# The v and attention-value projections as two 1024-column groups with seven block products in five tile pairs

## The chip, the cores and the metric

The kernel runs on one core of one Trainium2 chip. The metric is the device time of one execution, in microseconds (us). Before the change three runs took 1321.61, 1322.16 and 1323.86 us; the median is 1322.16.

The engines are named as the profile names them: PE is TensorE (matrix products), DVE is VectorE, ACT is ScalarE, POOL is GpSimd, and SP is SyncE, whose queue issues the loads of the weights. A letter q behind a name means the engine's issuing queue. An "L" and a number is a line of the kernel.

## The reference

One layer of an encoder over 256 positions with 2048 columns, all in float32:

```
h    = rms_norm(x) ; proj = h @ w_in              # u, v | q, k, va | gates A, B
y_a  = gelu(u) * (w_s @ LN(gelu(v)) + b_s)        # per 128-position chunk, 8 groups
y_b  = neighbourhood_attention(q, k, va)          # 16 heads of 64, 4 x 64 grid, learned bias
m    = sigmoid(gA) * (y_a @ w_branch[:1024]) + sigmoid(gB) * (y_b @ w_branch[1024:])
x    = x + m @ w_out
x    = x + conv_ffn(rms_norm(x))                  # up 2048 -> 11008, conv width 3, SiLU gate, down
out  = rms_norm(x)
```

The columns of `w_in` are u (0 to 1023), v (1024 to 2047), q, k, the attention values va (4096 to 5119), and the two gates of 2048 columns each. The change is about v and va: each is 256 x 2048 times 2048 x 1024.

## The kernel before

**Exact products from three.** A float32 product is made of three float32r matmuls. Each operand is split into a high part (a copy in float32r, by ACT) and a low part (operand minus high part, by DVE), and the product is high x high + low x high + high x low. For activations these parts lie in `h` (x chunks), `m`, `a`; for weights in `whi` and `wlo`. I call the three matmuls a triple.

**Pieces.** The weights of the whole layer are cut into pieces of 512 KB (128 partitions x 1024 values), numbered in the order in which PE uses them. SP loads them into `wraw`, five buffers deep (`LOAD_AHEAD`). `split_to` splits a piece: ACT copies it to `whi`, DVE subtracts for `wlo`, in four buffers each, three pieces ahead of PE (`SPLIT_AHEAD`).

**Order.** Nothing is scheduled by a tool: each engine executes its instructions in the order in which the Python code writes them. `begin(i)` opens piece i. It issues loads up to piece i + 4, writes the split of piece i + 3, and then runs the tasks that stand for i in a table (`at(i, f)`). For i below 5 the tasks come ahead of the splits. Then come the piece's matmuls. A task put at i thus stands behind the split of piece i + 3 and ahead of the split of piece i + 4 on ACT and DVE, and ahead of the matmuls of piece i on PE.

**Start.** x arrives in eight chunks of 256 columns (`load_x`, 256 KB each). `x_chunk(c)` turns one over on PE (four 128x128 transposes, L496), and ACT and DVE split it (L468, L475) into `h`. In the first eight pieces one chunk per piece is turned and used at once. The sums of squares of x (`x_stats`, on ACT) and the norm (`x_norm`) follow at pieces 5 to 9; the norm's factor is applied when a group is finished.

**Groups.** A `natural` group makes 512 output columns: eight pieces, each of two k tiles (k counts the 16 tiles of 128 input columns), for two halves of the positions, 12 matmuls a piece. A `stationary` group makes transposed outputs. A `wide` group makes 1024 columns in 16 pieces, each one k tile by two column halves: 2 x 2 triples a piece. In chosen pairs of k tiles (`quads`) the four sums of two products are made with seven triples instead of eight (a Winograd-type scheme): sums of activations (`act_sums`, L290 to L295, split at L301 and L302) and of weights (`weight_sums`, L308 to L311, split at L318 and L319) take the place of one triple. The weight sums stand at three pieces ahead of their use, their split two ahead. Four further banks P hold block products that are added to several outputs when the last pair is done (L807 to L811 for a gate), and the other four banks C are added when the group ends (L822). PSUM has eight banks in all.

**Before the change** v is two natural groups (pieces 0 to 15), then come u (16 to 31), and va, q and k, and half of the gates in alternating natural and stationary groups, among which the attention's small steps are hung as tasks. v's LayerNorm (`ln_stats`) hangs on pieces 17 and later, beside u. The gates' other halves, w_out and the down-projection are wide groups already.

Of the kernel before, what the change touches and what calls it, by code (L numbers as in the profile page):

```python
# [15 lines left out]
T = 256  # L16
# [26 lines left out]
GATE_QUADS = (1, 3, 5)  # L43
# [4 lines left out]
Y_GAP = 192  # L48
# [4 lines left out]
def trunk_kernel(ctx, tc, x, norm_mix, w_in, ln_g, ln_b, w_s, b_s, rpb, w_branch, w_out,  # L53
# [48 lines left out]
    def load_to(n):  # L102
        while n_loaded[0] < min(n, len(pieces)):
# [58 lines left out]
    midway = {}  # L162

# [66 lines left out]
    def run_group(g, by_block=0):  # L230
# [4 lines left out]
        for i in range(n0, n1 - by_block):  # L235
# [7 lines left out]
            for b in range(nblk):  # L243
                if b == 1 and i in midway:
                    midway.pop(i)()
                products(g, ps, i, b, h, l)
# [13 lines left out]
    def wide(src, row0, order, c0, acts, quads, room, done, sums=None):  # L260
        n0 = plan_wide(src, row0, order, c0)
        boxes = {}
        for q in quads:
            i = n0 + 2 * q
            whole[i] = whole[i + 1] = None
# [8 lines left out]
            at(i - 2, lambda b=b: weight_sums_split(b, room))  # L274
# [49 lines left out]
    def run_wide(g, tail=0):  # L324
# [12 lines left out]
        for i in range(n0, n1 - tail):  # L337
# [162 lines left out]
    yT = [ypool.tile([128, 2, T], F32R, name=f"y{k}") for k in range(KD)]  # L500
    ypool.tile([128, Y_GAP // 4], F32, name="gap")

# [6 lines left out]
    def ev_vg(j):  # L509
        def done(ps, i):  # L510
            if j == 0:
                at(i + 2, lambda: gelu_v(ps, i))
            else:
                gelu_v(ps, i)

        def gelu_v(ps, i):
            G = gm_pool["p"]
            if j == 0:
                gm_pool["v"] = [G.tile([128, GMW], F32, name=f"vg{t}") for t in range(NT)]
                gm_pool["sum"] = const.tile([128, NT, 2], F32, name="vsum")  # L520
            for t in range(NT):
                nc.scalar.activation(gm_pool["v"][t][:, j * 512:(j + 1) * 512], ps[t], AF.Gelu_apprx_tanh,
                                     scale=st1["r"][:, t:t + 1], accum_out=gm_pool["sum"][:, t, j:j + 1])
            if j == 1:
                at(i + 1, ln_stats)
        return done

    def ln_stats():
        i = cur[0]
        mu = const.tile([128, NT], F32, name="mu")  # L530
# [5 lines left out]
        nc.vector.tensor_add(mu, su[:, :, 0], su[:, :, 1])  # L536
        nc.vector.tensor_scalar(nm, mu, -1.0 / GMW, None, op0=OP.mult)
# [70 lines left out]
    def ev_va(j):  # L608
        def done(ps, i):
            A = at_pool["p"]  # L610
            va = A.tile([128, NT, 512], F32, name="va", bufs=1)
            for t in range(NT):
                nc.scalar.activation(va[:, t, :], ps[t], AF.Copy, scale=st1["r"][:, t:t + 1])

            def windows(r):
                for b in range(NBLK):
                    c0 = (r % 2) * 64 + WIN0[b]
                    nc.gpsimd.dma_start(at_pool["v"][r * WIN:(r + 1) * WIN, b, j * 512:(j + 1) * 512],
                                        va[c0:c0 + WIN, r // 2, :])

            for r in range(ROWS):
                at(i + 1 + r // 2, lambda r=r: windows(r))
        return done
# [177 lines left out]
    def ev_gate_sums(br):  # L801
        def done(P, i):
            def go():
                gate_tile(br)
                p1, p5, p6, p7 = P
                g11, g12, g21, g22 = (mg["t", br][:, t, c * 512:(c + 1) * 512] for t in range(2) for c in range(2))
                nc.scalar.activation(g11, p1, AF.Copy)  # L807
# [353 lines left out]
    for g in g_vg:  # L1161
        run_group(g)
# [108 lines left out]
```

## Time and profile before

| | us |
|---|---|
| median of three runs | 1322.16 |
| the profiled execution | 1321.89 |
| its span, first to last instruction | 1319.9 |
| PE busy in the span | 1307.3 (99%) |
| DVE busy | 1030.5 (78%) |
| ACT busy | 755.0 (57%) |
| POOL busy | 101.6 (8%) |

How to read the lines that follow. A row of the order in time has start, length, engine, line, operation, written tile <- read tiles, form, how many were merged (x4), and in brackets how long the engine sat idle before and what ended that. A row of waits has the waiting instruction, what it waited for, us in total, times, and the longest. A row of a stretch has its length and, for PE, weight loads, DVE, ACT and POOL, the busy time and number of instructions, then the granted clock of PE, the share of DMA, and GB/s. A row of a group has busy time and the mean in ns of one.

### The profile page before, as it was taken

The numbers are of one execution on the slowest core, as the hardware profiler recorded it, in microseconds if no ns is written. First come the engines' busy times: TensorE is split into PE (matmuls) and PEld (weight loads), VectorE is DVE, ScalarE is ACT, GpSimd is POOL, SyncE is SP. The second block draws the span as 40 slices with busy tenths as digits, with TensorE's granted clock in tenths as the row PEclk, the third lists the DMA queues.
The fourth block names the chain that finished last, engine by engine and source line by source line (L and its number), as shares of the span: only waits on it lengthen the run. The fifth ranks groups of instructions, "written<-read, shape, count | busy, mean of one in ns | idle before, by whom it ended". The sixth has DMA issues, their size and how long they took to land.

```text
span 1319.9 us, 19273 instructions
## 1 busy us (share of the span) xinstructions
PE 1307.3 (99%) x6791; PEld 1115.5 (85%) x6791; DVE 1030.5 (78%) x1561; ACT 755.0 (57%) x1127; POOL 101.6 (8%) x192
## 2 busy tenths in 40 slices
PE   9999999999999999999999999999999999999997
PEld 7888888888887888888888888888888888888885
DVE  6477667767598966996787878787878779999997
ACT  6565566667554644556655556565555556555653
POOL 0241155530000000000000000000000000000000
PEclk9999999999999999999999999999999999999999
DMA  9766775755666666665656665656566657656663
GB/s 317 231 189 183 216 224 165 218 173 155 199 176 208 200 197 221 219 214 162 191 179 195 184 194 181 202 176 204 180 195 187 192 154 229 220 192 206 212 197 122
DMA packets 174800, 259.37 MB, mean 197 GB/s; under 512 B 12920, under 2 KB 124400, under 8 KB 174704
## 3 DMA queue, kind: packets, MB, share of 16 engines
q1 hardware_dynamic: 170416, 250.31, 60.9%
q0 software_dynamic: 3968, 7.30, 2.2%
q8 instruction: 53, 0.87, 0.3%
q10 hardware_dynamic: 320, 0.53, 0.1%
q14 instruction: 43, 0.35, 0.1%
HBM read 253.90 MB, written 2.10 MB: 194 GB/s over the span
## 4 chain that ended last, share of the span: by engine, by line
PE 98%; DVE 1%; DMA 0%; ACT 0%; issue 0%; SPq 0%; ACTq 0%; DVEq 0%
PE bank L196 31%; PE bank L200 16%; PE bank L285 10%; PE bank L283 10%; PE bank L284 10%; PE bank L224 7%; PE bank L226 7%; PE bank L225 7%; PE bank L722 1%; DMA wraw<-in_w_in_dram 0%; PE bank L772 0%; PE bank L598 0%; PE bank L762 0%; PE bank L933 0%; PE bank L496 0%
## 5 line engine op out<-in xcount | busy, mean ns | idle before, releaser
L144 DVE TENSOR_TENSOR wlo<-wraw,whi 128x1024 fp32r<-128x1024 f32 (+1 forms) x471 | 553.6, 1186 | 225.6 <-ACT whi L143 120.9
L143 ACT ACTIVATE whi<-wraw 128x1024 fp32r<-128x1024 f32 (+1 forms) x471 | 475.3, 1022 | 225.9 <-PE bank L225 72.1
L196 PE MATMUL bank<-h,whi 128*128 128x512 f32 x1760 | 425.2, 392 | 0.0
L196 PEld LDWEIGHTS bank<-h,whi 128*128 128x128 f32 x1760 | 322.5, 189 | 61.6
L200 PEld LDWEIGHTS bank<-h,wlo 128*128 128x128 f32 x1760 | 225.9, 191 | 8.8
L200 PE MATMUL bank<-h,wlo 128*128 128x256 f32 x1760 | 228.6, 283 | 0.0
L958 ACT ACTIVATE tc<-ta,ck 128x256 f32<-128x256 f32 x86 | 47.1, 594 | 117.1 <-DVE ta L956 117.1
L224 PE MATMUL bank<-whi,h 128*128 128x512 f32 x256 | 102.4, 400 | 0.6 <-ACT whi L143 0.6
L285 PE MATMUL bank<-wlo,a 128*128 128x512 f32 x260 | 101.6, 391 | 0.2 <-DVE wlo L144 0.2
L283 PE MATMUL bank<-whi,a 128*128 128x512 f32 x260 | 101.3, 390 | 0.0
L284 PE MATMUL bank<-whi,a 128*128 128x512 f32 x260 | 101.3, 390 | 0.0
L225 PE MATMUL bank<-whi,h 128*128 128x512 f32 x256 | 100.1, 391 | 0.3 <-DVE h L475 0.3
L226 PE MATMUL bank<-wlo,h 128*128 128x512 f32 x256 | 100.2, 391 | 0.0
L285 PEld LDWEIGHTS bank<-wlo,a 128*128 128x128 f32 x260 | 48.8, 188 | 11.3 <-DVE wlo L144 1.3
L284 PEld LDWEIGHTS bank<-whi,a 128*128 128x128 f32 x260 | 48.9, 188 | 10.1
L283 PEld LDWEIGHTS bank<-whi,a 128*128 128x128 f32 x260 | 48.8, 188 | 10.1
L224 PEld LDWEIGHTS bank<-whi,h 128*128 128x128 f32 x256 | 48.3, 189 | 10.4 <-ACT whi L143 1.1
L226 PEld LDWEIGHTS bank<-wlo,h 128*128 128x128 f32 x256 | 48.1, 188 | 10.6 <-DVE wlo L144 0.4
L225 PEld LDWEIGHTS bank<-whi,h 128*128 128x128 f32 x256 | 48.2, 188 | 10.1 <-DVE h L475 0.8
L1234 POOL DMA_DIRECT2D gfin<-in_norm_final_dram x4 | 2.2, 548 | 696.8 <-DVE tc L969 577.3
L961 DVE SCALAR_TENSOR_TENSOR tc<-ta,ck,tc 128x255 f32<-128x255 f32 x86 | 41.4, 481 | 14.4 <-ACT tc L958 14.4
L948 ACT ACTIVATE tb<-bank 128x256 f32<-128x256 f32 x86 | 28.3, 385 | 42.5 <-PE bank L196 42.2
(254 smaller groups left out, 1702.4 us busy)
## 6 DMA issues: line engine op xcount, KB each, us to landing
wraw<-in_w_up_dram SPq DMA_DIRECT2D x336, 256.0 KB, 3.4
wraw<-in_w_in_dram SPq DMA_DIRECT2D x111, 512.0 KB, 4.3
wraw<-in_w_down_dram SPq DMA_DIRECT2D x86, 512.0 KB, 4.7
wraw<-in_w_in_dram SPq DMA_DIRECT2D x66, 256.0 KB, 3.5
wraw<-in_w_branch_dram SPq DMA_DIRECT2D x32, 512.0 KB, 3.9
wraw<-in_w_out_dram SPq DMA_DIRECT2D x32, 512.0 KB, 4.4
xs<-in_x_dram SPq DMA_DIRECT2D x8, 256.0 KB, 7.4
vw<-va POOLq DMA_DIRECT2D x32, 64.0 KB, 5.3
```

The source lines that it names most:

```text
L143: nc.scalar.activation(h[:, k, :m], w[:, k, :m], AF.Copy)
L144: nc.vector.tensor_sub(l[:, k, :m], w[:, k, :m], h[:, k, :m].bitcast(F32))
L196: nc.tensor.matmul(p, h[:, k - k0, b * 128:(b + 1) * 128], acts(k), start=k == 0, stop=k == nk - 1)
L200: nc.tensor.matmul(p[:, :T], l[:, k - k0, b * 128:(b + 1) * 128], acts(k)[:, 0, :], start=False, stop=False)
L224: nc.tensor.matmul(p, xh, h[:, kk, :m], start=st, stop=False)
L225: nc.tensor.matmul(p, xl, h[:, kk, :m], start=False, stop=False)
L226: nc.tensor.matmul(p, xh, l[:, kk, :m], start=False, stop=sp)
L283: nc.tensor.matmul(p, xh, h, start=st, stop=False)
L284: nc.tensor.matmul(p, xl, h, start=False, stop=False)
L285: nc.tensor.matmul(p, xh, l, start=False, stop=sp)
L958: nc.scalar.activation(v, u, AF.Identity, scale=ck[:, 1, ch:ch + 1], bias=ck[:, 3, ch:ch + 1])
L961: nc.vector.scalar_tensor_tensor(v[:, 1:], u[:, :T - 1], ck[:, 0, ch:ch + 1], v[:, 1:], op0=OP.mult, op1=OP.add)
```

## The change

v and va become wide groups of 16 pieces each and run first, one behind the other: v in pieces 0 to 15, va in 16 to 31, u in 32 to 47. v has its seven-product pairs at pieces 10 to 13 (`V_QUADS` 5 and 6), va at 18, 19, 22, 23, 26 and 27 (`VA_QUADS` 1, 3 and 5). The k tiles are taken in another order (`V_ORDER`, `VA_ORDER`), and the x chunks are turned at pieces 0 to 9 in the order of `X_TURN`, 0, 3, 1, 4, 2, 5, 6, 7. The first piece is one k tile, loaded as two column halves, and its first six matmuls use the first half alone. The sums of x chunks 1, 2 and 6 that the pairs need are made at pieces 3, 5 and 20 (`X_SUMS`).

The results of v and va are no longer taken from PSUM by ACT alone: `post_sums` and `add_sums` (DVE) combine the banks in SBUF, and ACT applies Gelu or the norm's factor there. v's LayerNorm falls on pieces 17 to 24. The turning of w_s and of the constants of later stages moves from pieces 14 to 19 to pieces 29 to 31, and the row factor `rb` from 12 to 29. The attention's fill now consists of gate groups; va's windows are copied by POOL in 16 transfers over all columns instead of 32 over half of them. The second gate group gets other pairs and k orders, and one more branch group stands ahead of the attention's end. The number of pieces stays the same.

```diff
-GATE_QUADS = (1, 3, 5)
+V_QUADS, V_ORDER = (5, 6), (0, 1, 6, 7, 8, 9, 10, 11, 12, 13, 2, 3, 4, 5, 14, 15)
+VA_QUADS, VA_ORDER = (1, 3, 5), (0, 1, 2, 3, 6, 7, 4, 5, 8, 9, 12, 13, 10, 11, 14, 15)
+X_TURN = ((0, 0), (3, 1), (1, 2), (4, 3), (2, 4), (5, 5), (6, 7), (7, 9))
+X_SUMS = ((1, 3, 3), (2, 5, 5), (6, 20, 20))
+GATE_PAIRS = (2, 4, 6)
+GATE_QUADS = ((2, 4, 6), (1, 3, 5))
...
             if i == 0:
                 for k in range(kn):
-                    if k:
-                        load_x(256, 256)
-                    nc.sync.dma_start(w[:, k, :cn], src[r0 + k * 128:r0 + (k + 1) * 128, c0:c0 + cn])
+                    nc.sync.dma_start(w[:, k, :cn], src[r0:r0 + 128, c0 + k * step:c0 + k * step + cn])
...
-                for t in range(NT):
-                    for c in range(2):
-                        plain(i, t, c)
+                for t, c in ((0, 0), (0, 1), (1, 0), (1, 1)) if i else ((0, 0), (1, 0), (0, 1), (1, 1)):
+                    plain(i, t, c)
...
+    def post_sums(P, x, spare):
+        p1, p5, p6, p7 = P
+        (x11, x12), (x21, x22) = x
+        nc.scalar.activation(x11, p1, AF.Copy)
+        nc.vector.tensor_add(spare, p6, x11)
+        nc.vector.tensor_add(x12, p5, spare)
+        nc.vector.tensor_add(x21, p7, spare)
+        nc.vector.tensor_add(x22, p5, x21)
+
+    def add_sums(ps, x):
+        for t in range(NT):
+            for c in range(2):
+                nc.vector.tensor_add(x[t][c], ps[t][c], x[t][c])
...
+    def ev_v(ps, i):
+        add_sums(ps, gm_pool["v4"])
...
+        at(i + 1, gelu)
+        at(i + 2, ln_stats)
...
-    g_vg = [natural(w_in2, 0, KD, V0 + j * 512, 512, xt, ev_vg(j)) for j in range(2)]
...
+    g_v = wide(w_in2, 0, V_ORDER, V0, xt, V_QUADS, first_room, (ev_v_sums, ev_v), first_sums,
+               lambda name, dt: s_room["odd"].tile([128, 2, 512], dt, name=name))
+    g_va = wide(w_in2, 0, VA_ORDER, VA0, xt, VA_QUADS, first_room, (ev_va_sums, ev_va), first_sums)
...
-    at(12, lambda: st1.__setitem__("rb", bcast_cols(st1["r"])))
+    at(29, lambda: st1.__setitem__("rb", bcast_cols(st1["r"])))
...
-    at(14, lambda: turn_ws(0))
-    at(15, lambda: turn_ws(1))
+    at(30, lambda: turn_ws(0))
+    at(31, lambda: turn_ws(1))
     preload[13] = [ld for ld, _ in late]
     for n, (_, f) in enumerate(late):
-        at(17 + n // 2, f)
+        at(29 + n // 2, f)
```

How the order moves, on three places. First DVE at the start. `wlo` is the low half of a piece, `h3` to `h5` are x chunks, `y0` and `y6` hold activation sums and their low half. Before, from the split of piece 3:

```order
L144 TENSOR_TENSOR wlo_252<-wraw_153,whi_251 128x1024
L475 SCALAR_TENSOR_TENSOR h4_113<-bank_270,gmix_85,h4_113 128x256 x2
L144 TENSOR_TENSOR wlo_280<-wraw_156,whi_279 128x1024
L475 SCALAR_TENSOR_TENSOR h5_114<-bank_297,gmix_85,h5_114 128x256 x2
L144 TENSOR_TENSOR wlo_307<-wraw_212,whi_306 128x1024
```

Changed, from the split of piece 3 to that of piece 4:

```order
L148 TENSOR_TENSOR wlo_230<-wraw_138,whi_229 128x1024
L291 TENSOR_TENSOR y0_248<-h1_110 128x512
L293 TENSOR_TENSOR y0_248<-y0_248 128x128
L294 TENSOR_TENSOR y0_248<-y0_248 128x128
L295 TENSOR_TENSOR y0_248<-y0_248 128x128
L296 TENSOR_TENSOR y0_248<-y0_248 128x128
L303 TENSOR_TENSOR y6_254<-y0_248,y6_254 128x512
L475 SCALAR_TENSOR_TENSOR h4_113<-bank_257,gmix_85,h4_113 128x256 x2
L148 TENSOR_TENSOR wlo_267<-wraw_141,whi_266 128x1024
```

Six instructions moved in between two splits; a second set stands between the split of piece 8 and chunk 5. The next place is DVE behind the split of piece 17 (`vg` is v, `y0` and `y1` the weight sums, `wsT` the turned w_s). Before:

```order
L144 TENSOR_TENSOR wlo_554<-wraw_533,whi_553 128x1024
L1153 COPY wsT_138<-bank_557 128x512
L144 TENSOR_TENSOR wlo_578<-wraw_551,whi_577 128x1024
L1153 COPY wsT_138<-bank_581 128x512
L144 TENSOR_TENSOR wlo_604<-wraw_575,whi_603 128x1024
```

Changed, from the split of piece 17 over the half split of piece 18 to the first of the last adds:

```order
L148 TENSOR_TENSOR wlo_574<-wraw_553,whi_573 128x1024
L522 TENSOR_TENSOR junk_75<-bank_509,vg0_577 128x512
L523 TENSOR_TENSOR vg0_577<-bank_508,junk_75 128x512
L524 TENSOR_TENSOR vg1_578<-bank_510,junk_75 128x512
L525 TENSOR_TENSOR vg1_578<-bank_508,vg1_578 128x512
L148 TENSOR_TENSOR wlo_599<-wraw_571,whi_598 128x512
L309 TENSOR_TENSOR y0_602<-wraw_571 128x512
L310 TENSOR_TENSOR y1_603<-wraw_596,y0_602 128x512
L311 TENSOR_TENSOR y0_602<-wraw_596,wraw_571 128x512
L312 TENSOR_TENSOR y1_603<-wraw_596,y1_603 128x512
L530 TENSOR_TENSOR vg0_577<-bank_173,vg0_577 128x512
```

The first adds, the weight sums and the last adds (the first of four is shown, then comes the split of piece 19) now stand between these splits. The third place is ACT at v's LayerNorm; `junk` is the target of the squares (L542, now L563), `vg` of the normalisation (L552, now L573). Before, beside u:

```order
L542 ACTIVATE junk_75,vs4_634<-vg0_475,nmu_632 128x512 x2
L143 ACTIVATE whi_666<-wraw_619 128x1024
L542 ACTIVATE junk_75,vs4_634<-vg1_476,nmu_632 128x512 x2
L143 ACTIVATE whi_688<-wraw_664 128x1024
L448 ACT_TABLE_LOAD
```

Changed, beside va; `whi_704` is the half copy of piece 22:

```order
L563 ACTIVATE junk_75,vs4_684<-vg0_577,nmu_682 128x512 x2
L147 ACTIVATE whi_704<-wraw_676 128x512
L563 ACTIVATE junk_75,vs4_684<-vg1_578,nmu_682 128x512 x2
L147 ACTIVATE whi_730<-wraw_702 128x1024
L319 ACTIVATE y2_734<-y0_708 128x1024
L319 ACTIVATE y3_738<-y1_709 128x1024
L302 ACTIVATE y8_748<-y0_742 128x512
```

The squares kept their place between copies, and behind them the copies of the weight sums and the sums of chunk 6 have joined.

More of the change, by code (lines that the diff above doesn't have):

```diff
@@ L255, in run_group, with wide @@
             done(ps, b)
-    def wide(src, row0, order, c0, acts, quads, room, done, sums=None):
+    def wide(src, row0, order, c0, acts, quads, room, done, sums=None, odd=None):
         n0 = plan_wide(src, row0, order, c0)
         boxes = {}
-        for q in quads:
+        for n, q in enumerate(quads):
             i = n0 + 2 * q
+            own = odd if odd and n % 2 else room
             whole[i] = whole[i + 1] = None
@@ L804, in go @@
                 gate_tile(br)
-                p1, p5, p6, p7 = P
-                g11, g12, g21, g22 = (mg["t", br][:, t, c * 512:(c + 1) * 512] for t in range(2) for c in range(2))
-                nc.scalar.activation(g11, p1, AF.Copy)
-                nc.vector.tensor_add(junk, p6, g11)
-                nc.vector.tensor_add(g12, p5, junk)
-                nc.vector.tensor_add(g21, p7, junk)
-                nc.vector.tensor_add(g22, p5, g21)
+                mg["x", br] = [[mg["t", br][:, t, c * 512:(c + 1) * 512] for c in range(2)] for t in range(NT)]
+                post_sums(P, mg["x", br], junk)
             at(i + 1, go)
@@ L1115, in trunk_kernel @@
     at(0, lambda: keep_awake(WAKE[1]))
[L1116 to L1118 removed]
+    for c, i in X_TURN[1:]:
+        at(i, lambda c=c: x_chunk(c))
     xsq = const.tile([128, NT, 4], F32)
```

157 lines of the change are left out of this document (79 added, 78 removed).

## The prediction

> **What bounds the kernel now.** I read the page first (span, busy shares, chain), then what TensorE (PE) waited for, then stretches of the span, and last the order in time of the engines. The page:
>
> ```profile
> span 1319.9 us, 19273 instructions
> ...
> PE 1307.3 (99%) x6791; PEld 1115.5 (85%) x6791; DVE 1030.5 (78%) x1561; ACT 755.0 (57%) x1127; POOL 101.6 (8%) x192
> ...
> PE 98%; DVE 1%; DMA 0%; ACT 0%; issue 0%; SPq 0%; ACTq 0%; DVEq 0%
> ```
>
> TensorE is busy for 99% and carries 98% of the chain that ended last. What it waited for (us in total, times, longest):
>
> ```profile
> PE bank L433 <- POOL ident masks.py:199: 1.4, 1, 1.4
> PE bank L283 <- DVE m L473: 0.9, 1, 0.9
> PE bank L224 <- ACT whi L143: 0.6, 1, 0.6
> PE bank L225 <- DVE h L475: 0.3, 1, 0.3
> ```
>
> The first belongs to the start-up. So a matmul less shortens the run, as long as VectorE (DVE) and ScalarE (ACT) deliver in time. How full DVE is depends on the stage:
>
> ```profile
> 66.00:99.00 33.00, 33.00 (x200) 29.49 (x199) 26.31 (x43) 21.14 (x31) 15.11 (x23) 1.00 0.64 189
> ...
> 429.00:462.00 33.00, 33.00 (x147) 27.35 (x146) 31.31 (x37) 21.03 (x23) 0.00 (x0) 1.00 0.65 200
> ```
>
> The columns after the length are PE, weight loads, DVE, ACT, POOL. In the seven-product gate groups (429 to 462) DVE works 31.3 of 33 us and PE still never waits. That is the closest row to what the change asks for.
>
> **The change, step by step.** *Less on PE.* Five pairs need 7 instead of 8 triples: 5 x 3 = 15 matmuls of 512 columns fewer. Their pace, and the pieces around it:
>
> ```profile
> 8.28 0.51 PE L224 MATMUL bank<-whi,h 128*128 128x512 f32 x1 [0.61 <-ACT whi L143]
> ...
> 14.38 0.60 PE L496 MATMUL bank<-ident,xs 128*128 128x128 f32 x4
> 14.73 0.48 PE L224 MATMUL bank<-whi,h 128*128 128x512 f32 x1
> ...
> 17.60 0.60 PE L496 MATMUL bank<-ident,xs 128*128 128x128 f32 x4
> ...
> 28.32 0.50 PE L225 MATMUL bank<-whi,h 128*128 128x512 f32 x1 [0.29 <-DVE h L475]
> ...
> 28.89 0.39 PE L224 MATMUL bank<-whi,h 128*128 128x512 f32 x1
> ...
> 44.31 0.39 PE L226 MATMUL bank<-wlo,h 128*128 128x512 f32 x1
> ```
>
> From 28.89 to 44.31 lie 68 steps: 0.227 us each, 2.72 for a piece of 12; the four transposes of an x chunk add 0.35 (14.38 to 14.73), and a piece with its chunk takes 3.22 (14.38 to 17.60). Gain: 15 x 0.227 = 3.4. The wait of 0.61 before the second half of piece 0 goes too: six matmuls, not three, now run on the first half, and no x chunk is loaded between the halves. Together **-4.0**. The 0.29 at 28.32 says that an x chunk arrives with no lead at this stage.
>
> *More on DVE and ACT.* Durations, DVE first:
>
> ```profile
> 16.84 1.23 DVE L144 TENSOR_TENSOR wlo<-wraw,whi 128x1024 fp32r<-128x1024 f32 x1
> ...
> 22.30 0.88 DVE L475 SCALAR_TENSOR_TENSOR h<-bank,gmix,h 128x256 fp32r<-128x256 f32 x2 [1.02 <-ACT h L468]
> 23.25 4.63 DVE L144 TENSOR_TENSOR wlo<-wraw,whi 128x1024 fp32r<-128x1024 f32 x4
> ...
> 38.59 0.15 DVE L1128 TENSOR_REDUCE ss<-xsq 128x2 f32<-128x8 f32 x1
> ...
> 40.01 0.16 DVE L453 TENSOR_TENSOR n_r<-n_r,n_s 128x2 f32<-128x2 f32 x1
> ...
> 76.13 1.32 DVE L556 TENSOR_TENSOR vg<-vg,lng 128x1024 f32<-128x1024 f32 x1
> ...
> 78.63 1.32 DVE L144 TENSOR_TENSOR wlo<-wraw,whi 128x1024 fp32r<-128x1024 f32 x1
> ...
> 370.15 0.68 DVE L290 TENSOR_TENSOR t<-h 128x512 f32<-128x512 f32 x1
> ...
> 371.81 1.22 DVE L144 TENSOR_TENSOR wlo<-wraw,whi 128x1024 fp32r<-128x1024 f32 x1
> ...
> 385.84 0.69 DVE L144 TENSOR_TENSOR wlo<-wraw,whi 128x512 fp32r<-128x512 f32 x1
> ...
> 388.98 1.28 DVE L837 TENSOR_TENSOR g<-bank,g 128x512 f32<-128x512 f32 x2
> ...
> 392.51 2.36 DVE L319 TENSOR_TENSOR l<-t,h 128x1024 fp32r<-128x1024 f32 x2
> ...
> 420.30 0.69 DVE L808 TENSOR_TENSOR junk<-bank,g 128x512 f32<-128x512 f32 x1
> ...
> 422.35 0.69 DVE L811 TENSOR_TENSOR g<-bank,g 128x512 f32<-128x512 f32 x1
> ...
> 432.47 2.48 DVE L822 TENSOR_TENSOR g<-bank,g 128x512 f32<-128x512 f32 x4
> ```
>
> ```profile
> 22.15 3.90 ACT L143 ACTIVATE whi<-wraw 128x1024 fp32r<-128x1024 f32 x4
> 25.95 0.83 ACT L468 ACTIVATE h<-bank,gmix 128x256 fp32r<-128x256 f32 x2
> ...
> 63.92 0.73 ACT L542 ACTIVATE junk<-vg,nmu 128x512 f32<-128x512 f32 x1 [3.99 <-DVE nmu L537]
> ...
> 64.77 0.72 ACT L542 ACTIVATE junk<-vg,nmu 128x512 f32<-128x512 f32 x1
> ...
> 72.77 1.25 ACT L552 ACTIVATE vg<-vg,nmr,ln_r 128x1024 f32<-128x1024 f32 x1 [0.76 <-DVE nmr L548]
> ...
> L301 ACT ACTIVATE h<-h 128x512 fp32r<-128x512 f32 x14 | 8.9, 633 | 38.6 <-PE bank L285 18.8 <-DVE h L295 14.4 <-DVE wlo L144 3.2
> ```
>
> Step from one DVE instruction to the next: split of a piece 1.14 ((4.63 - 1.23) / 3), an x chunk 0.80, activation sums 1.66 (370.15 to 371.81) plus 0.60 after ACT's 0.63 copy, a half split with its four weight sums 3.14 (385.84 to 388.98), the split of these sums 2.27, the first adds of a finished group 2.66 (420.30 to 422.35, and 0.61), its last adds 2.40, the norm chain 1.6 (38.59 to 40.17), one affine 2.50. ACT: a copy 0.95 ((3.90 - 1.05) / 3), half a copy 0.54 (0.63 less the same overlap), an x chunk 0.73.
>
> *Piece 4* (first order fence). The activation sums now stand between the splits of pieces 3 and 4, and x chunk 4 waits for them on ACT. Call T the start of the transposes ahead of piece 3. Before, the split of piece 3 ends at T + 0.47 (17.60, and 16.84 + 1.23), and I keep that. The sums end at T + 2.1, ACT's copy of them, chunk 4 and the copy of piece 4 (0.54 + 0.73 + 1.05) at T + 4.4, the low half 1.2 later, T + 5.6. PE wants the high half at T + 3.57 (3.22 + 0.35) and, held up by 0.85 there, the low half at T + 4.95: 0.85 + 0.65 = **+1.5**. Queued behind on both engines are chunk 2 and the splits of pieces 5 to 8.
>
> *Piece 6* is the first that uses x chunk 5, which now stands behind five splits and a second set of sums. From S, the start of piece 4's low half: 1.14 + 0.80 + 4 x 1.14 + 1.74 = 8.25, ACT 0.54 and 0.47: S + 9.3. PE has done pieces 4 and 5 at S + 1.23 + 2.3 + 0.35 + 2.72 = S + 6.6. The delay of 2.7 and another 0.4 for the chunk's low half: **+3.1**.
>
> *Piece 8* needs chunk 6, behind the half split and weight sums of piece 10. ACT comes to that half copy after piece 9's and two squares of x (as long as L542's, 0.85): S + 12.8; with 3.14 and 0.47 the chunk's low half is there at S + 16.5. PE, restarted at S + 10.0, wants it at S + 15.8 (11 matmuls, 0.35, 2.72, one matmul): **+0.7**.
>
> *Pieces 8 to 26* (second and third fence). PE and DVE stand together at chunk 6, without lead. Up to the end of the split of piece 27, which piece 26 needs, DVE has 13 splits 14.8, four half splits with sums 12.6, four splits of sums 9.1, chunks 1.2, norm 1.6, first adds 2.7, last adds 2.4, activation sums with ACT's copy 2.9, LN's small chain 2.0 (norm and two more), two affines 5.0: 54.3. It also waits for ACT: 2.3 where LN's squares (2 x 0.85) and half a copy (0.63) come first, 1.0 where a normalisation does (1.15 + 0.95, less the 1.14 of the split before), and by estimate 0.3 behind x's squares. Sum 57.9. PE has in the same stretch 11 + 12 + 84 (four pairs of 21) + 96 + 5 = 208 matmuls, 47.2, and 0.35 of transposes: 47.6. The lead of three pieces that hides this in the gate groups never builds up here: **+10.3**, most of it before pieces 24 and 26.
>
> *Piece 29* asks for three more of the eight PSUM banks while the group holds all eight; they come free with the third of the first adds. DVE: 2.27 + 4 x 1.14 + 2.05 = 8.9 after that split, PE arrives after 28 matmuls and four transposes, 6.7: **+2.2**.
>
> *Nothing* for attention: its cover is the absence of any PE wait there, and the POOL copies of v are half as many and issued some 30 pieces ahead of their first reader. If late, they would hold the first weighted sum. Gates keep their count of products; with DVE up to 95% full there I bound the moved sums by -0.9 (the wait on L473, if it goes) and +0.9 (if one like it joins), and take 0.
>
> Sum: -4.0 + 1.5 + 3.1 + 0.7 + 10.3 + 2.2 = **+13.8**. The profiled execution took 1321.89 (1319.9 of it in the span), 0.3 below the median 1322.16: 1335.7 on the one, **1336** on the other.
>
> **A rule weighed.** The gate row above shows a DVE at 95% that holds nobody up. The Trainium skill, Perfetto Trace Analysis, "Identifying the Most-Contended Engine", says to take the engine with the highest occupancy and relieve it first. By the whole-run shares that is PE, and the sum would be -4.0; by the same rule read for pieces 8 to 26 it is DVE, 57.9 against 47.6. That page itself warns, under "Optimization Strategy", that the most contended engine changes with the regime; the rows side with that.
>
> **Rivals.** *DVE keeps up* as in the gate groups, and only the gain is left: 1318.2. For it speaks the row at 429 to 462; against it that those groups start with three pieces of lead and carry neither x chunks nor LN. It decides if the shortfalls together fall below 4.0 instead of 17.8. Chance 0.07, of which 0.02 near no change.
> *ACT's waits vanish* because copies slip in while DVE is behind, and piece 29 finds its banks: 1336 - 3.6 - 2.2 = 1330. Chance 0.10.
> *Loads come late*: raw buffers are kept until the sums have read them. Before, a load takes
>
> ```profile
> wraw<-in_w_in_dram SPq DMA_DIRECT2D x111, 512.0 KB, 4.3
> ```
>
> from issue to landing; one of these fully on the path would give 1340. Against: five buffers, and DVE is the later one anyway. Chance 0.08.
> *The clock drops* after the longest wait, some 5 us before piece 26. Before has no such wait, so no row prices it: at half pace the next 28 matmuls would cost 6.4, of which piece 29's 2.2 are swallowed: between 1336 and 1340, I say 1338. Chance 0.11. The Trainium skill, TensorE: Matmul & The Clock Gate, Part 1, gives a window of about 3.4 us of idleness after which the clock halves; by it I estimate 1.7 lost, which piece 29 would swallow. The granted clock is 1.00 in the rows above, and no run here shows such a drop.
>
> **How the numbers follow.** My case has 0.64, at 1336 (5% on the 57.9 would move it by 2.9). Range 1329 to 1342: it leaves out DVE keeping up and the far ends. Within 0.2% (2.6 us, what a measurement here can tell) I put 0.02, faster 0.05, slower 0.93.
>
> **What would show it.** PE waits for the high copies and splits by DVE at the L284 to L286 lines near 21, 30, 38, 83 and 96 us, and for a bank near 103; DVE 90% busy or more from 33 to 99; the rest of the run as before but shifted. Wrong if PE has no wait over 1 us before 110, or if new waits appear in attention or in the gates.

## The result and the profile after

The changed kernel took 1338.24 us (median of four runs, 1335.82 to 1338.68) against 1322.01 beside it: a ratio of 1.0116, with a 95% interval of 1.0099 to 1.0134. Four more executions, among the experiments below, gave 1335.69, 1335.82, 1336.44 and 1338.54 (ratio 1.0104, 1.0088 to 1.0121). The median of all eight is 1337.31, and I compare the experiments with that. The forecast was 1336 in a range of 1329 to 1342. The executions lie in two groups 2.4 us apart; more on that under the clock.

The profiled execution of the changed kernel took 1335.82 us, with a span of 1334.0. Its page:

```profile
span 1334.0 us, 19330 instructions
...
PE 1307.7 (98%) x6776; PEld 1112.1 (83%) x6776; DVE 1067.0 (80%) x1624; ACT 765.1 (57%) x1138; POOL 89.4 (7%) x176
...
PE 90%; DVE 6%; ACT 2%; issue 2%; DMA 0%; SPq 0%; ACTq 0%; DVEq 0%
```

PE has 15 matmuls fewer and is as long busy as before. Its share of the chain fell from 98% to 90%; DVE and ACT now hold 8%. What PE waited for (us in total, times, longest):

```profile
PE bank L286 <- DVE wlo L148: 7.0, 8, 3.6
PE bank L284 <- ACT whi L147: 3.9, 2, 3.1
PE bank L284 <- ACT h L468: 2.2, 1, 2.2
PE bank L433 <- POOL ident masks.py:199: 1.4, 1, 1.4
PE bank L407 <- DVE y L524: 1.1, 1, 1.1
PE bank L285 <- DVE h L475: 1.1, 2, 0.7
PE bank L407 <- DVE junk L522: 0.3, 1, 0.3
```

Apart from the start-up's 1.4 they add up to 15.6 us, where before had 2.0: 0.9, 0.6, 0.3, and one of 0.2 near the end that both have. Where they lie, told by stretches of the span (length; busy PE, weight loads, DVE, ACT, POOL; granted clock; share of DMA; GB/s), first of before and then of after:

```profile
0.00:110.00 110.00, 107.53 (x558) 91.04 (x559) 70.49 (x115) 68.83 (x115) 23.20 (x44) 1.00 0.75 236
```

```profile
0.00:110.00 110.00, 94.06 (x414) 74.63 (x415) 89.50 (x135) 68.29 (x103) 1.32 (x8) 0.98 0.67 222
110.00:400.00 290.00, 290.00 (x1627) 247.28 (x1626) 203.85 (x323) 176.65 (x290) 83.02 (x160) 1.00 0.64 189
```

In the first 110 us DVE has 19 us more to do and PE works 13.5 us less. Behind that, PE is busy without a gap through the attention. PE's order of time, with the waits that the terms of the prediction speak of (near 83 us is piece 24, near 96 piece 26) and those in the gates:

```profile
10.95 0.50 PE L286 MATMUL bank<-wlo,h 128*128 128x512 f32 x1 [0.53 <-DVE wlo L148]
...
21.10 0.50 PE L284 MATMUL bank<-whi,h 128*128 128x512 f32 x1 [0.75 <-ACT whi L147]
...
22.35 0.50 PE L286 MATMUL bank<-wlo,h 128*128 128x512 f32 x1 [0.53 <-DVE wlo L148]
...
30.36 0.49 PE L284 MATMUL bank<-whi,h 128*128 128x512 f32 x1 [2.23 <-ACT h L468]
...
38.19 0.50 PE L285 MATMUL bank<-whi,h 128*128 128x512 f32 x1 [0.70 <-DVE h L475]
...
76.36 0.50 PE L286 MATMUL bank<-wlo,h 128*128 128x512 f32 x1 [0.43 <-DVE wlo L148]
...
79.89 0.39 PE L286 MATMUL bank<-y,h 128*128 128x512 f32 x1
83.41 0.50 PE L284 MATMUL bank<-whi,h 128*128 128x512 f32 x1 [3.13 <-ACT whi L147]
83.74 0.40 PE L285 MATMUL bank<-whi,h 128*128 128x512 f32 x1
84.82 0.80 PE L286 MATMUL bank<-wlo,h 128*128 128x512 f32 x1 [0.68 <-DVE wlo L148]
85.41 0.63 PE L284 MATMUL bank<-whi,h 128*128 128x512 f32 x1
85.84 0.63 PE L285 MATMUL bank<-whi,h 128*128 128x512 f32 x1
...
87.85 0.39 PE L284 MATMUL bank<-whi,h 128*128 128x512 f32 x1
...
96.18 0.50 PE L286 MATMUL bank<-wlo,h 128*128 128x512 f32 x1 [3.60 <-DVE wlo L148]
...
421.77 0.50 PE L286 MATMUL bank<-wlo,h 128*128 128x512 f32 x1 [0.52 <-DVE wlo L148]
...
426.03 0.50 PE L286 MATMUL bank<-wlo,h 128*128 128x512 f32 x1 [0.56 <-DVE wlo L148]
```

Two things are to be seen. First, a listed wait is a little less than what it costs: from 79.89 to 83.74 there are two steps, 3.85 us, where 0.45 would do; that is 3.40 for a wait listed as 3.13, so about 0.27 is to be added to each (the wait of 0.70, between the matmuls at 37.10 and 38.52, gives the same). Second, between 84.8 and 87.7 the steps are 0.43 us and not 0.227: PE ran at half its clock. The clock's part is told below, since it turned out to be part of the result.

### The profile page after: what moved, and what is told of

Read it like the earlier page. It is cut to its first block, busy times and chain, and to the rows that moved or that the text cites. A ratio compares the mean times of both kernels' runs of the same rounds, so it can differ in the third digit from the quotient of the medians.

```text
span 1334.0 us, 19330 instructions
## 1 busy us (share of the span) xinstructions
PE 1307.7 (98%) x6776; PEld 1112.1 (83%) x6776; DVE 1067.0 (80%) x1624; ACT 765.1 (57%) x1138; POOL 89.4 (7%) x176
## 4 chain that ended last, share of the span: by engine, by line
PE 90%; DVE 6%; ACT 2%; issue 2%; DMA 0%; SPq 0%; ACTq 0%; DVEq 0%
PE bank L198 30%; PE bank L202 16%; PE bank L286 10%; PE bank L285 10%; PE bank L284 10%; PE bank L226 4%; PE bank L227 4%; PE bank L228 4%; DVE wlo L148 2%; ACT whi L147 1%; PE bank L753 1%; DMA wraw<-in_w_in_dram 0%; PE bank L803 0%; PE bank L619 0%; PE bank L793 0%
## 5 line engine op out<-in xcount | busy, mean ns | idle before, releaser
L285 PE MATMUL bank<-whi,a 128*128 128x512 f32 x260 | 101.2, 389 | 0.0
L286 PE MATMUL bank<-wlo,h 128*128 128x512 f32 x204 | 80.9, 397 | 6.8 <-DVE wlo L148 6.8
L284 PE MATMUL bank<-whi,h 128*128 128x512 f32 x204 | 81.4, 399 | 6.1 <-ACT whi L147 3.9
L285 PE MATMUL bank<-whi,h 128*128 128x512 f32 x204 | 80.4, 394 | 1.1 <-DVE h L475 1.1
L285 PEld LDWEIGHTS bank<-whi,a 128*128 128x128 f32 x260 | 48.8, 188 | 10.1
L286 PEld LDWEIGHTS bank<-wlo,h 128*128 128x128 f32 x204 | 38.7, 190 | 17.7 <-DVE wlo L148 9.9
L284 PEld LDWEIGHTS bank<-whi,h 128*128 128x128 f32 x204 | 38.7, 190 | 15.0 <-ACT whi L147 4.7
L226 PE MATMUL bank<-whi,y 128*128 128x512 f32 x128 | 50.5, 394 | 0.0
L226 PE MATMUL bank<-whi,h 128*128 128x512 f32 x128 | 50.4, 394 | 0.0
```

What stands on the lines that cost most here:

```text
L226: nc.tensor.matmul(p, xh, h[:, kk, :m], start=st, stop=False)
L284: nc.tensor.matmul(p, xh, h, start=st, stop=False)
L285: nc.tensor.matmul(p, xl, h, start=False, stop=False)
L286: nc.tensor.matmul(p, xh, l, start=False, stop=sp)
```

## The experiments

The theory on trial is the prediction's: from piece 4 to piece 29 the weight sums, activation sums, first and last adds and LayerNorm give DVE, with ACT in front of it, more to do than PE has, and what is over is added to the time. Rivals are named with each run.

### Where it comes from: undoing the pairs

*All five pairs plain.* The wide groups, their order of blocks and x chunks and the gates stay as changed; `copy_sums` copies the four banks to SBUF by DVE, for va as for v.

```diff
-V_QUADS, V_ORDER = (5, 6), ...
-VA_QUADS, VA_ORDER = (1, 3, 5), ...
-X_SUMS = ((1, 3, 3), (2, 5, 5), (6, 20, 20))
+V_QUADS, V_ORDER = (), ...
+VA_QUADS, VA_ORDER = (), ...
+X_SUMS = ()
...
-        add_sums(ps, gm_pool["v4"])
+        copy_sums(ps, gm_pool["v4"])
```

> The two 1024-column groups stay, with their order of blocks and x chunks, but all five seven-product pairs become plain ones (8 block products): no activation or weight sums and no first adds; the last adds become copies by VectorE from PSUM. Gates as changed. Theory (the sums and adds on VectorE are the price): 15 matmuls come back (+3.4 us), the waits between 21 and 96 us go, and the time is near that of the kernel before, 1322 to 1324. Rival (the groups, their order of blocks and the changed turn of the x chunks cost the time by themselves): the gain of 3.4 us is lost and the waits stay, 1338 to 1342.

1322.10 us against 1322.29: a ratio of 1.000 (0.9991 to 1.0009). So the regrouping costs nothing on balance, and the pairs, with the sums and adds that they bring, are the whole price. Of PE's waits in this profile these are left, beside the start-up's:

```profile
PE bank L286 <- DVE wlo L148: 1.5, 4, 0.6
...
PE bank L285 <- DVE h L475: 1.0, 2, 0.7
```

*v's two pairs plain* (`V_QUADS = ()`, v copied out by DVE, activation sums of chunks 1 and 2 at pieces 10 and 12), and *va's three pairs plain* (`VA_QUADS = ()`, va copied out by DVE, no sums of chunk 6):

> The two seven-product pairs of v (pieces 10 to 13) become plain ones, v's group is copied out of PSUM by VectorE, and the activation sums of pairs 1 and 2, which va's pairs still need, are made at pieces 10 and 12. The three pairs of va stay. Theory (the shortfall of VectorE adds up from piece 4 on): the waits at pieces 4 and 6 go, six matmuls come back (+1.4 us), VectorE loses two half splits' weight sums, their splits and one set of first adds (about 11 us of its own work), and the time falls by 3 to 7 us to 1330 to 1335; a wait of 3 to 5 us before piece 26 stays. Rival (va's pairs alone make the price): the time stays at 1336 to 1338. Second rival (v's pairs alone make it): 1322 to 1324.

> The counterpart to v without pairs: v keeps its two seven-product pairs and the early activation sums, va's three pairs become plain ones and va is copied out of PSUM by VectorE; layer norm stays where the change puts it. Theory (VectorE's shortfall is paid where it arises, and VectorE catches up where nothing is added): against the kernel before, six matmuls and the wait in piece 0 go (-2.0 us), the waits at pieces 4, 6 and 8 stay (1.3, 2.6, 0.7 us) with at most 1.8 us for a stretch at half clock near 32 us; none over 0.5 us between 60 and 110 us: 1323.5 to 1327. Rival (v's pairs leave VectorE behind for the rest of both groups, so layer norm and the splits of va come late even without pairs there): waits of 2 us or more between 60 and 100 us, 1328 to 1333.

Without v's pairs 1332.23 us, without va's 1327.43. The former lies in the range that the theory gave, the latter 0.4 above its range. Without va's pairs no wait is left between 60 and 110 us, so DVE does catch up where nothing is added. The prices add: 5.1 for v's pairs and 9.9 for va's are 15.0, and all five together cost 15.2 (1337.31 less 1322.10). That is closer than single executions of the changed kernel agree (1335.69 to 1338.68), so the last tenths are chance.

### What it hangs on: the amount of DVE's work

*LayerNorm of v 15 pieces later*, beside u:

```diff
-        at(i + 2, ln_stats)
+        at(i + 17, ln_stats)
```

> The layer norm of v (two squares a block, small chain, two normalisations, two affines) starts at piece 33 instead of piece 18, so it stands beside the u groups. Theory (from piece 8 on VectorE has more to do than TensorE, and what it does beyond that is added to the time): VectorE loses about 7 us of its own work (two affines 5.0, small chain 2.0) and some 3 us of waiting for ScalarE between pieces 16 and 27; the waits near 83 and 96 us shrink from 7.8 us together to under 1.5 us, and the time falls by 8 to 10 us to about 1329 (1326 to 1331). The waits near 21, 30 and 38 us stay as they are. Rival (the waits near 83 and 96 us come from the weight sums themselves, which stand late in the order, and layer norm only fills gaps): the time stays within 2 us of 1338.

1327.44 us, 9.9 less, without a change in a single product. The two long waits of 3.13 and 3.60 near 83 and 96 us are gone. LayerNorm's squares and normalisations leave ACT too, so this run alone doesn't say which of the two engines was short; the dose below is on DVE alone. The two largest groups of the waits that are left, beside which stand 1.1, 0.7 and 0.6 us:

```profile
PE bank L286 <- DVE wlo L148: 2.9, 6, 0.6
PE bank L284 <- ACT h L468: 2.2, 1, 2.2
```

*Activation sums three pieces later*, which takes nothing off DVE:

```diff
-X_SUMS = ((1, 3, 3), (2, 5, 5), (6, 20, 20))
+X_SUMS = ((1, 6, 6), (2, 8, 8), (6, 20, 20))
```

> The activation sums of pair 1 move from piece 3 to piece 6 and those of pair 2 from piece 5 to piece 8, behind the x chunks and splits that they held up. Nothing is taken away. Rival (each wait has its own cause and price): the waits near 21 and 30 us, 1.3 and 2.6 us, go, and the time falls by about 4 us to 1334. Theory (VectorE's whole work from piece 4 to piece 27 is the price, and an early wait only pays part of it in advance): the early waits go, those near 83 and 96 us grow by as much or more, and the time stays within 1 us of 1338 or rises by up to 4 us.

1338.51 us, 1.2 more than unmoved. The waits at 21 and 30 us go, as both views expected, and the time doesn't fall. In their place x chunk 6 is late, which neither view had named; the theory's guess that the waits near 83 and 96 us would grow was wrong, they stayed at 3.1 and 3.6:

```profile
PE bank L286 <- DVE wlo L148: 7.1, 8, 3.6
PE bank L285 <- DVE h L475: 3.9, 3, 2.8
```

*A dose of 4.6 us on DVE*, once in va's group (pieces 20 and 21, as shown) and once in u's (44 and 45):

```diff
+DOSE = {20: 2, 21: 2}
...
+            for _ in range(DOSE.get(i, 0)):
+                nc.vector.tensor_sub(l[:, :kn, :m], w[:, :kn, :m], h[:, :kn, :m].bitcast(F32))
             split_t[i] = (h, l)
```

> The low half of the splits of pieces 20 and 21 (va group) is computed three times instead of once: four more VectorE instructions of 1.14 us a step, 4.6 us in all, on the same operands, so the result is the same. Theory (VectorE has no spare time from piece 8 to piece 27): the whole dose is added to the time, 4 to 5.5 us over the changed kernel (1336 to 1338), so 1340.5 to 1343, and the wait before piece 24 or in piece 26 grows by about as much. Rival (VectorE stands still there for lack of ScalarE's copies or of loads, and only the order of its work counts): it would be absorbed, and the time stays within 1.5 us of the changed kernel's.

> The same four instructions, 4.6 us, now at pieces 44 and 45 in the second u group. Theory (there VectorE has slack and the splits run three pieces ahead): the time stays within 1 us of the changed kernel's, 1336 to 1338. Rival (any instruction added to VectorE costs its own length, wherever it stands): 4.6 us more, 1340.5 to 1343.

In va's group 1342.16 us: 4.9 more for 4.6 us of work. In u's 1338.85: 1.5 more, 0.85 above the range that the theory gave. There the trace shows one new wait of PE, 0.3 us; the other 1.2 are no more than single executions of the changed kernel differ (1335.69 to 1338.68). Both profiles, like the one of 1338.54 us below, have three drops of the clock; against that one the doses cost 3.7 (1342.21) and 0.8 (1339.35). The same instruction costs most or all of its length in the one place and little in the other.

*GpSimd in DVE's place* for the weight sums:

```diff
+        e = nc.gpsimd if i < 32 else nc.vector
-        nc.vector.tensor_sub(t13[:, 0], r0[:, 1], r0[:, 0])
+        e.tensor_sub(t13[:, 0], r0[:, 1], r0[:, 0])
...
```

> The four weight sums of each of the five v and va pairs (20 instructions of 512 columns, 2.4 us a pair on VectorE) are done by GpSimd, which is busy for 7% of the run; everything else is as changed. No run so far shows how long GpSimd takes for one; the nearest row is its select on 64x256 at 0.7 us, so 1 to 3 us each, 4 to 12 us a pair, one pair at a time. Theory (VectorE's work is the price, whoever takes it): VectorE is relieved of 12 us; if GpSimd needs under 5 us a pair, ScalarE's copies of the sums come in time, the waits near 83 and 96 us shrink to under 3 us together and the time falls by 4 to 8 us to 1329 to 1333. If GpSimd needs more, ScalarE waits for it in order, the copies behind it come late and the time rises above 1338; then the trace shows ScalarE released by GpSimd. Rival (the price is the order in which ScalarE and VectorE take turns, not their amount of work): no fall whatever GpSimd's speed.

1340.09 us, 2.8 more. GpSimd takes 1.28 us for a sum while DVE is idle (the first row), and about 2.2 beside DVE's splits; from the first to the last sum a pair takes 5 to 9 us, beyond the 5 from which the theory expected a loss. The expected way of it is there, ACT waits 2.9 us in all for GpSimd's sums. But it is not the only one: DVE itself becomes slower. Rows of POOL and of DVE in this kernel:

```profile
33.72 1.28 POOL L312 TENSOR_TENSOR y<-wraw 128x512 f32<-128x512 f32 x1
...
69.92 2.15 POOL L311 TENSOR_TENSOR y<-wraw,y 128x512 f32<-128x512 f32 x1
72.03 2.27 POOL L312 TENSOR_TENSOR y<-wraw 128x512 f32<-128x512 f32 x1
```

```profile
68.61 4.54 DVE L148 TENSOR_TENSOR wlo<-wraw,whi 128x1024 fp32r<-128x1024 f32 x2
...
87.32 1.13 DVE L453 TENSOR_SCALAR ln_s<-ln_s 128x2 f32<-128x2 f32 x1
```

and the same two of DVE in the changed kernel:

```profile
66.98 2.57 DVE L148 TENSOR_TENSOR wlo<-wraw,whi 128x1024 fp32r<-128x1024 f32 x2
...
83.03 0.17 DVE L452 TENSOR_SCALAR ln_s<-ln_s 128x2 f32<-128x2 f32 x1
```

Two splits take 4.54 us and not 2.57, and an operation on 128x2 values takes 1.13 us and not 0.17, about the length of one GpSimd sum. DVE lost the 20 sums, 12 us, and is busy for 1067.3 us as against 1067.0. So nothing was taken off DVE's time. The Trainium skill, SBUF — State Buffer, "SBUF: two separate sides", says that DVE and GpSimd share a pair of ports, which one instruction holds to its end while the other waits; these rows agree. The run therefore doesn't test the theory, whose condition was a relieved DVE; it shows that GpSimd isn't a relief here.

### The clock

*The changed kernel once more*, unedited:

> The changed kernel once more, nothing edited. The profile of the changed kernel took 1335.82 us with a mean granted clock of 0.997, its other three executions 1338.18 to 1338.68 with 0.993. Theory (the clock drops after long waits, and in some executions more than once): executions lie in two groups, near 1335.8 and near 1338.3, and a longer one shows a second or third stretch of 3.4 us at a granted clock of 0.5, each worth about 1.5 us where no later wait swallows it. Rival (the 2.4 us are ordinary scatter of the time): executions spread evenly between 1335 and 1339, and none shows more than the one stretch of reduced clock at 84 to 88 us.

Three executions lie at 1335.69 to 1336.44 and one, the profiled, at 1338.54; with the first four, four lie near 1336 and four near 1338.4. The times stand in two groups, as expected, but the number of drops alone doesn't make them: the three short executions here have a mean granted clock of 0.994 or 0.995, less than the 0.997 of the first profile with its nearly equal time. Where their drops lie is not shown. The longer one (0.993), by stretches:

```profile
28.35:31.76 3.41, 0.83 (x2) 0.48 (x3) 2.61 (x8) 2.25 (x5) 0.00 (x0) 1.00 1.00 328
31.76:35.18 3.42, 3.42 (x9) 2.63 (x8) 1.24 (x2) 1.39 (x5) 0.00 (x0) 0.50 0.84 340
...
82.97:86.38 3.41, 0.73 (x2) 0.30 (x2) 2.65 (x10) 3.13 (x4) 0.00 (x0) 1.00 0.00 0
86.38:89.79 3.41, 3.20 (x8) 2.52 (x9) 2.33 (x3) 3.41 (x5) 0.00 (x0) 0.50 0.53 154
...
93.21:96.62 3.41, 1.30 (x6) 0.75 (x4) 3.38 (x4) 2.73 (x3) 0.00 (x0) 1.00 0.51 142
96.62:103.44 6.82, 5.48 (x13) 4.33 (x14) 6.82 (x7) 3.65 (x5) 0.00 (x0) 0.50 0.39 105
```

Before its last microseconds, where PE has no work left, the clock was halved three times, for 3.41, 3.41 and 6.82 us, against once (84.28 to 87.69) in the first profile. The starts lie 16.0 and 3.0 times 3.413 us apart, so the decision falls on a grid of that step; in the fourteen traces of this case all 19 such drops last one or two steps of it. Ahead of each drop stands one step of the grid in which PE was busy for 0.73 to 1.30 us of 3.41. Whether a wait is punished depends on how it lies on the grid, as two stretches of the first profile show (the grid laid through its drop at 84.28):

```profile
80.87:84.28 3.41, 0.73 (x2) 0.30 (x2) 2.60 (x10) 3.11 (x5) 0.00 (x0) 1.00 0.00 0
84.28:87.69 3.41, 2.87 (x7) 2.32 (x8) 2.33 (x3) 3.41 (x5) 0.00 (x0) 0.50 0.49 149
...
91.11:94.52 3.41, 1.47 (x7) 0.89 (x5) 3.38 (x5) 2.41 (x3) 0.00 (x0) 1.00 0.42 102
94.52:97.93 3.41, 1.75 (x8) 1.44 (x9) 3.41 (x4) 3.19 (x4) 0.00 (x0) 1.00 0.35 87
```

The wait of 3.13 us lies within one step and costs a drop; the longer one of 3.60 is shared by two steps, each with 1.47 us or more of work, and costs none. Laid through the clock's changes in each of the fourteen traces, the grid puts the limit between 1.45 us of work (in LayerNorm late, 26.75 to 30.16; followed by half clock, like every step at full clock with less) and these 1.47, which is 42 to 43% of a step as the trace models PE's time.

*Worthless matmuls in PE's waits.* A weight of zeros is multiplied and added to a running sum, which leaves the result as it is:

```diff
+FILL = {6: 9, 24: 12, 26: 14}
...
+            for _ in range(FILL.get(i, 0)):
+                nc.tensor.matmul(C[0][0], zero, x_pairs[0][:, 0].rearrange("p a t -> p (a t)"), start=False, stop=False)
```

> 35 more matmuls of 512 columns with a weight of zeros, added to a running sum: 9 ahead of piece 6, 12 ahead of piece 24, 14 ahead of piece 26, 8.0 us of TensorE work placed where TensorE waits for VectorE and ScalarE; one small VectorE instruction makes the zeros. Theory (TensorE has that time to spare, and a long idle stretch is followed by 3.4 us or more at half clock): the time does not rise; the granted clock is 1.00 up to the last 10 us, and as the slow matmuls are gone the time falls by 0 to 3 us to 1333.5 to 1336, with less scatter. Rival (the work of TensorE is the bound and is paid in full): 8 us more, 1344 to 1346. Second rival (the half clock has another cause than idleness): the time stays at 1336 to 1338.5 and the stretches at half clock, near 32, 86 and 97 us, stay.

1334.85 us, and four executions within 0.15 us (1334.78 to 1334.93): 8 us more work on PE, and 2.5 us less time. The first 110 us in this kernel, in the columns of the stretches:

```profile
0.00:110.00 110.00, 101.69 (x454) 80.86 (x455) 90.78 (x139) 68.24 (x103) 1.32 (x8) 1.00 0.67 222
```

PE is busy 7.6 us longer than in the changed kernel, and the clock is whole. This shows both that PE isn't the bound there and that the halved clock came from its waits. How lost clock is paid through DVE can be seen at the drop near 32 us of the longer execution: ACT's copy of the first half of piece 10 needs one of the four `whi` buffers, and so waits for the slow matmuls of piece 6 (the profile names L285). The low half by DVE, with all that stands behind it, starts at the copy's end, at 34.52 and 36.28; the transposes of x chunk 6, which stand behind the same matmuls, end at the same time. The row of ACT in the two profiles of the changed kernel, first without and then with that drop:

```profile
33.85 0.63 ACT L147 ACTIVATE whi<-wraw 128x512 fp32r<-128x512 f32 x1 [0.87 <-PE bank L285]
```

```profile
35.62 0.63 ACT L147 ACTIVATE whi<-wraw 128x512 fp32r<-128x512 f32 x1 [2.44 <-PE bank L285]
```

PE's rows tell where the 2.7 us between the two spans (1336.7 and 1334.0) arise. The longer execution is 0.2 us behind at piece 6 (30.55 against 30.36) and 1.8 behind at piece 8 (39.96 against 38.19) and at piece 26 (97.96 against 96.18), so the drop near 32 us costs 1.6. At piece 29 it is 2.75 behind (107.75 against 105.00) and stays so: the drop of 6.82 us costs only 1.0 more, for it swallows the two waits for banks, 1.4 us, which are missing from this profile.

*The same with LayerNorm late* (nine such matmuls ahead of piece 6 alone):

> Layer norm late, and 9 matmuls with a weight of zeros ahead of piece 6, in its wait of 2.2 us; the only stretch at half clock of the version without them was at 30 to 37 us, after that wait. Theory (that stretch delays the transposes of the next x chunk, and all that VectorE does behind it): it goes, and the time falls from 1327.4 us by 1 to 3.4 us to 1324 to 1326.5, with executions closer together. Rival (lost clock is made good by the waits that follow, since VectorE is late anyway): the time stays at 1326.5 to 1328.

1326.18 us, 1.3 less than without them, and no stretch at half clock before the end. It is the theory's side, at its weak end; of the four executions without them one, with a granted clock of 0.998, took 1326.35.

### A version made from the findings

v without pairs, copied out by ACT; two pairs in va instead of three, with late activation sums; LayerNorm late; the pairs of both gate groups at the same, later places.

```diff
-V_QUADS, V_ORDER = (5, 6), ...
-VA_QUADS, VA_ORDER = (1, 3, 5), ...
-X_TURN = ((0, 0), (3, 1), (1, 2), (4, 3), (2, 4), (5, 5), (6, 7), (7, 9))
-X_SUMS = ((1, 3, 3), (2, 5, 5), (6, 20, 20))
+V_QUADS, V_ORDER = (), tuple(range(16))
+VA_QUADS, VA_ORDER = (2, 5), (0, 1, 6, 7, 2, 3, 8, 9, 10, 11, 4, 5, 12, 13, 14, 15)
+X_TURN = ((0, 0), (1, 1), (2, 2), (3, 3), (4, 5), (5, 7), (6, 9), (7, 11))
+X_SUMS = ((1, 10, 10), (2, 12, 12))
...
-GATE_QUADS = ((2, 4, 6), (1, 3, 5))
+GATE_QUADS = ((3, 5, 6), (3, 5, 6))
...
-        at(i + 2, ln_stats)
+        at(i + 17, ln_stats)
...
-    at(29, lambda: st1.__setitem__("rb", bcast_cols(st1["r"])))
+    at(15, lambda: st1.__setitem__("rb", bcast_cols(st1["r"])))
```

> A version made from the findings: v's group has no seven-product pair and is copied out by ScalarE; va has two pairs (third and sixth place) whose activation sums are made at pieces 10 and 12, behind the x chunks; x chunks 1 to 7 stand in order at pieces 1, 2, 3, 5, 7, 9, 11; layer norm starts at piece 33; the row factors are spread out at piece 15, not 29; both gate groups have their pairs at the fourth, sixth and seventh place, with their activation sums four pieces apart. Theory (seven-product pairs pay only where VectorE has room for them): 6 matmuls fewer than the kernel before (-1.4 us), no wait over 1 us between 8 and 110 us, no stretch at half clock before the last 10 us: 1319.5 to 1321.5, below the kernel before. Rival (two pairs in va are enough to make VectorE late): waits of 2 us or more near 90 us, and 1322 to 1326.

1320.20 us (median of eleven) against 1322.29: a ratio of 0.9984, 0.9975 to 0.9993. It is faster than both kernels, by 2.1 us than the one before. Its stretches from 33 to 99 us:

```profile
33.00:66.00 33.00, 33.00 (x152) 27.34 (x152) 23.76 (x40) 24.01 (x39) 0.62 (x2) 1.00 0.65 214
66.00:99.00 33.00, 33.00 (x152) 27.09 (x151) 24.80 (x32) 14.50 (x16) 0.00 (x0) 1.00 0.63 205
```

PE never waits there, with DVE at 24 to 25 of 33 us. Six matmuls fewer are 1.4 us; the waits of before at 8.28 and 28.32 us, which this profile doesn't have, would be as much again, so that the 2.1 is somewhat less than the two together. This version changes several things at once and shows that they fit together, not what each is worth.

## Why the prediction was right, and where it was not

The direction, the place and the size held: DVE's work in pieces 4 to 29 is the price (the pairs plain, the dose, LayerNorm moved), and nothing was paid in the attention. Two of the prediction's own signs failed. DVE was to be 90% busy or more from 33 to 99 us: it was 93% busy up to 66 and 84% from there on, where it waited for ACT. And new waits in the gates were to show it wrong: there are two, of 0.52 and 0.56. They are small, but "nothing in the gates" did not hold. By terms, each wait of the first profile with 0.27 added:

| step of the prediction | forecast | measured |
|---|---|---|
| matmuls saved | -3.4 | -3.4 (6776 against 6791) |
| waits of before at 8.28 and 28.32 us gone | -0.6 | -1.4 |
| piece 1's low half (0.53) | none | +0.8 |
| piece 4 (0.75 and 0.53) | +1.5 | +1.8 |
| piece 6 (2.23 and 0.39) | +3.1 | +3.2 |
| piece 8 (0.70) | +0.7 | +1.0 |
| pieces 8 to 26: waits (0.43, 3.13, 0.68, 3.60) | +10.3 | +8.9 |
| the same stretch: seven steps at half clock | in a rival | +1.3 |
| piece 29's banks (0.3 and 1.1) | +2.2 | +1.4 to 1.9 |
| gates (0.52 and 0.56, less 0.9 of before) | 0 | +0.5 |
| sum | +13.8 | +14.1 to 14.6 |

For the banks the lower figure is the waits as listed, the upper with the 0.27 for each. The span grew by 14.1 us (1334.0 less 1319.9).

*The stretch of pieces 8 to 26* was forecast as 57.9 us of DVE, with waits of 2.3 and 1.0 us for ACT in it. PE's row at 38.19 above gives its start, and DVE's rows its end and those waits:

```profile
71.94 0.69 DVE L148 TENSOR_TENSOR wlo<-wraw,whi 128x512 fp32r<-128x512 f32 x1 [2.31 <-ACT whi L147]
...
85.85 1.23 DVE L148 TENSOR_TENSOR wlo<-wraw,whi 128x1024 fp32r<-128x1024 f32 x1 [1.08 <-ACT whi L147]
...
94.91 1.22 DVE L148 TENSOR_TENSOR wlo<-wraw,whi 128x1024 fp32r<-128x1024 f32 x1
```

From 38.19 to the end of the split of piece 27 at 96.13 are 57.9 us. The term of 10.3 therefore held as a whole, and a slower PE could not change it: part of what the forecast gave to waits went into slow matmuls.

*The mis-sized steps.* Piece 1's wait of 0.53 (0.16 in the second profile) was not seen: PE reaches its low half earlier, now that piece 0 has no wait. The wait at 28.32 of before was read but not credited. The fit of the sum is thus partly luck: 0.8 too little saved and 0.8 overlooked cancel. The gates' moved sums cost 0.5, within the bounds given. The clock is the larger piece of luck: my case left it out, and without its drops (the filled waits, 1334.85) the forecast of 1336 would have been 1.1 too high.

*The rivals.* "DVE keeps up" fell. "ACT's waits vanish" fell: they came out at 2.31 and 1.08, and the banks were waited for. "Loads come late" fell: of PE's waits only 0.2 us is for a load, at the start, as before, and neither ACT nor DVE waits for one between 20 and 110 us. "The clock drops" came true in part, and not instead of my case but on top of it: the version with filled waits shows 1334.85 for the waits alone, and the median of all eight executions lies 2.5 above that. The forecast gave it 2 us after one wait near piece 26; it came after the wait of piece 24 in the first profile and after those of pieces 6, 24 and 26 in the second, where it swallowed piece 29's waits as the rival had said. Its page, TensorE: Matmul & The Clock Gate, Part 1, of the Trainium skill, speaks of an idle window of about 3.4 us that runs freely. The traces agree with the free-running grid of 3.41 us; they go further in that a step with 1.30 us of work (38%), in another trace 1.45 (42%), was still followed by half clock, and one with 1.47 us (43%) was not. The rival's remark that no run showed such a drop was not quite so: in the trace of before the granted clock is 0.50 from 1316 to 1320 us, but PE has no work left there, so no row could price it.

The rule weighed, to relieve the engine of highest occupancy, would have misled by whole-run shares: PE is at 98%, its weight loads at 83%, DVE at 80%, and PE could take 8 us more work for nothing in the stage that counts.

What stays open: why a drop lasts 3.41 us in some places and 6.82 in others (a step at half clock with 2.87 us of work, 84.28 to 87.69 in the first profile, was followed by the whole clock, one with 3.07, 30.16 to 33.57 in LayerNorm late, was not); where the drops of the short executions with a clock of 0.994 lie; and 1.2 of the 1.5 us that the dose cost beside u.

## What to carry to other kernels

An edit that trades matmuls for vector work is priced in the stage where it stands: add up the vector engine's work there against TensorE's between two points where both meet, and don't take a later, busier-looking stage as proof that it fits, if that stage enters with a lead. Waits that are caused by a queue that is behind move when the order is changed, and go only when work leaves the stage. Check whether the engine that is to take the work shares something with the one that is relieved.

## What was unexpected of the hardware

- Half clock doesn't need a wait of 3.4 us: 2.2 us ahead of piece 6 were enough in some executions, while 3.60 us ahead of piece 26 went free in one, by their place on a grid of 3.413 us. Two executions of one kernel so differ by up to 3.0 us, and the number of drops alone doesn't decide it: with a mean granted clock of 0.997 one took 1335.82, with 0.994 to 0.995 three took 1335.69 to 1336.44.
- Matmuls without use made the kernel 2.5 us faster and its four executions agree within 0.15 us.
- DVE's operation on 128x2 values took 1.13 us instead of 0.17 beside a GpSimd sum, and GpSimd's sum 2.15 to 2.27 instead of 1.28 beside DVE.
